# A two-layer encoder in split fp32 on one core: half of the first feed-forward group made by seven products instead of whole blocks, the forms of h made beside four blocks, and the last norm's weights scaled later

## The chip, the core and the metric

The kernel runs on one core of a Trainium2 chip. The metric is the device time of one execution in microseconds, as the median over runs; lower is better. Engines are named as the profile names them: PE (matmuls; PEld loads its stationary operand), DVE (elementwise), ACT (activations and copies), POOL (GpSimd, which here raises powers and issues the DMAs that add to what lies in memory) and SP (which issues most of the loads).

## The reference

There are two layers on x of 512 tokens by 1024 features, float32:

```python
h = rmsnorm(x, attn_norm[l]); proj = h @ w_in[l]          # 1024 -> 3072
... stick-breaking heads and differential heads ...        # mixed: 512 x 1024
x = x + mixed @ w_o[l]
h = rmsnorm(x, mlp_norm[l])
u = square(relu(h @ w_ff1[l]))                             # 1024 -> 4096
x = x + u @ w_ff2[l]                                       # 4096 -> 1024
```

After both layers comes one more `rmsnorm(x, final_norm)`. The change touches the feed-forward part (the last three lines) and the final norm.

## The kernel before

**Precision.** Every operand of a large product is split into two float32r parts, hi and lo: `hi = ACT copy(src)`, then `lo = DVE src - hi`. One product is three matmuls (`three`, L296 to L299): hi·hi, lo·hi and hi·lo. So each 512 KB tile of weights costs one ACT instruction (`whi`, L115) and one DVE instruction (`wlo`, L131) before PE can finish with it. All weight units stand in one list in the order of use (`_UNITS`); `W.next` hands out the next one and has later ones split ahead of their use.

**The feed-forward part** goes over four groups (`GROUPS`) of eight blocks of 128 hidden features in each layer. A group has two steps.

*First product, h·w_ff1.* In groups 1 to 3 it goes by seven products instead of eight: `quad_group(g, j)` runs once for each half j of the group. It takes quarters of h (256 tokens by 512 features) and quarters of the weights, or sums of these, in the order `FORMS = ("11", "x3", "x2", "21", "x1", "x4", "22")`, and each form is 24 matmuls of 128x256 into banks called X, V and Y. In group 0 of each layer the first product is made whole, by eight blocks `f0` to `f7` of 24 matmuls of 128x512 each. The reason in the code is that the forms of h (`hx`, sums and differences of quarters of h: x3, x2, 22, and x1 written over a quarter of h itself) are made only there: `h_form(k)` is called after block k, for k from 1 to 7, and `evict_whole` takes each block through relu and square and makes the seven forms of u for the second product.

*Second product, u·w_ff2.* It goes by seven products in all groups, with 128x512 matmuls into X, V, Y and W.

**Loads for the first product by seven.** `bring(n, role)` loads the quarters of half-group n. Role "a" is quarter 11, "b" is 12, "c" is 22, "d" is 21; role "e" is 12 with 22 added by a second DMA, which POOL issues with accumulation when the first has landed:

```python
quads = {"a": ("11",), "b": ("12",), "c": ("22",), "d": ("21",), "e": ("12", "22")}[role]
for q in quads:
    at = w1[_FIRST.index((l, g, j, q))]
    if q == quads[0]:
        nc.sync.dma_start(spots[role], at)
    else:
        nc.gpsimd.dma_start(spots[role], at, accum_op=ALU.add)
```

Tile `norms` holds role "e"; it also holds the sum of squares of x from which the norm before the feed-forward part is taken (`rms_square`: four transposes on PE, `rs_m`, three matmuls into the second block). Tile `waves` holds role "d". When form x3 has been split, DVE adds a to b and e to a (`add`, 128x1024 each), which gives the weights of x1 and x2.

**Order.** A scheduler that works with its own estimate of times puts the instructions of each engine in order when the program is built; each engine then runs its queue strictly in that order and waits where a semaphore asks for it. PE's queue may so hold matmuls of a later bank between those of an earlier one.

**In the last layer** `forth` transposes x back (four transposes and an ACT copy for each of eight pieces) beside the blocks of group 0, and the weights of the final norm are loaded into `gf` (two tiles of x) during form x3 of the last group's second product. `gf` is scaled by ACT (L1247, L1248, L1249) when the code has come to form x2 of that product; where these stand in ACT's queue is the scheduler's choice.

Of the kernel before, what the change touches and what calls it, by code (L numbers as in the profile page):

```python
# [12 lines left out]
AF = mybir.ActivationFunctionType  # L13
ALU = mybir.AluOpType
# [5 lines left out]
D = 1024  # L20
L = 2
# [3 lines left out]
GROUPS = 4  # L25
# [25 lines left out]
def _unit_list():  # L51
    units = []
    def qk(l, cq, ck, b):
        units.append(("p", l, cq + b * P))
        units.append(("p", l, ck + b * P))

    for l in range(L):
        for item in ORDER:
            b = int(item[1])
            if item[0] == "d":  # L60
                units.append(("x", l, b, 0))
                units.append(("x", l, b, 1))
            elif item[0] == "s":
                qk(l, SBQ, SBK, b)
            else:
                for half in range(2):
                    units.append(("v", l, (SBV if item[0] == "u" else DFV) + b * P, half))
        for half in (1, 0):
            for j in range(4):
                units.append(("o", l, half, j))  # L70
        for g in range(GROUPS):
            if g == 0:
                units.extend(("1", l, f) for f in range(2 * GP))
            else:
                units.extend(("s", l, g, j, form) for j in range(2) for form in FORMS)
            for form in FORMS2:
                for c in range(GP // 2):
                    units.append(("f", l, g, form, c))
    return units
# [9 lines left out]
_FIRST = [(l, g, j, q) for l in range(L) for g in range(1, GROUPS) for j in range(2) for q in QUADS]  # L89


class _Weights:
# [71 lines left out]
def trunk(ctx, tc, opened, xT, w, w2, w1, gfin, lamv, cos, sin, out):  # L164
# [168 lines left out]
    for l in range(L):  # L333
# [502 lines left out]
        with ExitStack() as fctx:  # L836
# [35 lines left out]
            groups = [(g, j) for g in range(1, GROUPS) for j in range(2)]  # L872
            spots = {"d": kept[(2, 1)], "e": norms.rearrange("p a t -> p (a t)")}
            serves = {"a": ("11", "x2"), "b": ("x1",), "c": ("22",), "d": ("21", "x4"), "e": ("x3",)}

# [48 lines left out]
            for g in range(GROUPS):  # L924
                for c in range(GP // 2):
# [20 lines left out]

            def evict_whole(pt, k):
                pair, which = k // 2, k % 2
                F = spots["de"[pair % 2]].rearrange("p (a t) -> p a t", a=4)
# [12 lines left out]
                split(hi[:, 3:5, :], lo[:, 3:5, :], F[:, 0:2, :])  # L962
                split_less(hi[:, 5, :], lo[:, 5, :], F[:, 2, :])
                split(hi[:, 6, :], lo[:, 6, :], F[:, 3, :])
# [11 lines left out]
                        op0=ALU.mult, op1=op)  # L976

            def h_form(k):
                if k == 1:
                    for c in range(4):  # L980
                        nc.scalar.activation(ta[:, c, :], x[:, c, early], AF.Copy, scale=gcol("mlp", l, c))
                    scaled(tb_, 0, late_, ta, ALU.subtract)
                elif k == 2:
                    scaled(tc_, 4, early, ta, ALU.subtract)
                    split(*h_forms["x3"], tb_)
                elif k == 3:
                    scaled(ta, 0, late_, tc_, ALU.add)
                elif k == 4:
                    scaled(tb_, 4, late_, ta, ALU.subtract)
                    split_less(*h_forms["x2"], ta)  # L990
                elif k == 5:
                    split_less(*h_forms["22"], tb_)
                elif k == 6:
                    for c in range(GP // 2):
                        fetch(0, "x3", c)
                elif k == 7:
                    split(*h_forms["x1"], tc_)
                    for c in range(GP // 2):
                        fetch(0, "21", c)

            def temp(k, name):
                if k == 3:
# [8 lines left out]
            def quad_group(g, j, banks_):  # L1011
# [8 lines left out]
                for form in FORMS:  # L1020
# [36 lines left out]
                    if j and form in ("11", "x3", "x2"):  # L1057
# [110 lines left out]
            for g in range(GROUPS):  # L1168
# [5 lines left out]
                    quad_group(g, 1, (s_, r_, q_))  # L1174
                    rest_of_forms(1, "21")
                else:
                    for k in range(2 * GP):
                        for n, pt in enumerate(block(f"f{l}_{g}_{k}", "any")):
                            if (k, n) == (1, 0):
                                rms_square(ssq, f"m{l}")  # L1180
                        evict_whole(pt, k)
                        h_form(k)
                        if last and k > 3:
                            for tb in (2 * (k % 2), 2 * (k % 2) + 1):
                                forth(tb, 1 - k // 6)
                    p_, q_, r_, s_ = ring[0] % 3, 3, (ring[0] + 1) % 3, (ring[0] + 2) % 3
                    held_on = {"Y": [bank("t", f"Y{l}{r}") for r in range(2)], "V": [bank("mm", f"V{l}{r}") for r in range(2)]}
                chains = {"X": [temp(k, f"X{l}{g}{k}") for k in (p_, q_)], **held_on}
                for form in FORMS2:
# [48 lines left out]
                    if g and form in ("11", "x3"):  # L1238
                        rest_of_forms(1, "x2" if form == "11" else "22")
                    if end and not last and form in ("21", "x2"):  # L1240
                        for c in range(4 * (form == "x2"), 4 * (form == "x2") + 4):
# [2 lines left out]
                        for c in range(2):  # L1244
                            nc.sync.dma_start(gf[c], gfin[512 * c : 512 * c + 512].partition_broadcast(P))
                    if end and last and form == "x2":
                        nc.scalar.activation(gf[0], gf[0], AF.Copy, scale=math.sqrt(D))  # L1247
                        nc.scalar.activation(gf[1], gf[1], AF.Copy, scale=-math.sqrt(D))  # L1248
# [101 lines left out]
```

## Time and profile before

| | |
|---|---|
| runs | 1136.55, 1139.55, 1139.09 us; median 1139.09 |
| the profiled execution, own time | 1138.57 us |
| its span | 1136.5 us, so 2.1 us lie around it |
| mean granted PE clock | 0.996 |
| busy: PE, DVE, ACT, POOL | 99%, 81%, 60%, 12% |
| group 0 of layer 0, first product | from 241.3 to 285.3 us of the span |
| group 0 of layer 1, first product | from 799.2 us; eight blocks with 32 transposes between them |

The timeline's rows are: start in us from the span's start, duration in us, engine, line, operation, what it writes and reads, shapes, how many were merged (x1), and in brackets the idle time before it with what ended that. The rows of a window are: the stretch, its length, each engine's busy time with the number of instructions, the granted PE clock, the share of the DMA engines' time and GB/s. The page's rows of DMA issues give the size of one and the median time from issue to landing.

### The profile page before, as it was taken

What the parts mean: (1) busy time and instruction counts of PE and PEld (TensorE: products, weight loads), DVE (VectorE), ACT (ScalarE), POOL (GpSimd) and SP (SyncE); (2) the same over time, 40 slices, a digit from 0 to 9 for tenths busy, and PEclk for the clock granted to TensorE, in tenths of its full rate; (3) what the DMA queues carried; (4) which work ended last, traced back from release to release, by engine and by line L of the source; (5) the groups of instructions that cost most, each with busy time, mean ns of one, the idle gap of its engine ahead of it and who ended that gap; (6) DMA issues with size and microseconds to landing.
All of it is one profiled execution on the core that took longest, in us unless ns stands there. A gap on an engine that the chain in (4) does not pass through costs nothing.

```text
span 1136.5 us, 17656 instructions
## 1 busy us (share of the span) xinstructions
PE 1122.4 (99%) x6613; PEld 992.6 (87%) x6613; DVE 914.9 (81%) x1329; ACT 687.0 (60%) x1115; POOL 137.5 (12%) x221
## 2 busy tenths in 40 slices
PE   9999999999999999999999999999999999999996
PEld 7899889888899899898888998988888998988975
DVE  7898788788669879779788877887877797797886
ACT  6456666567558457476345565675774574764763
POOL 1001343101001001001000014330010010010000
PEclk9999999999999999999999999999999999999998
DMA  7665353266877657738227544512487577567261
GB/s 250 149 187 147 93 168 112 74 207 161 234 195 165 173 163 168 204 110 224 75 78 206 162 131 130 159 65 75 167 198 199 159 167 204 149 154 216 78 128 75
DMA packets 59317, 174.99 MB, mean 154 GB/s; under 512 B 7264, under 2 KB 8544, under 8 KB 59232
## 3 DMA queue, kind: packets, MB, share of 16 engines
q1 hardware_dynamic: 50160, 141.84, 39.9%
q0 software_dynamic: 8640, 31.46, 15.8%
q8 instruction: 52, 0.85, 0.3%
q10 hardware_dynamic: 432, 0.56, 0.1%
q14 instruction: 33, 0.27, 0.1%
HBM read 144.47 MB, written 4.19 MB: 131 GB/s over the span
## 4 chain that ended last, share of the span: by engine, by line
PE 88%; DVE 5%; DMA 2%; issue 2%; ACT 1%; SPq 1%; POOL 0%; POOLq 0%; DVEq 0%; ACTq 0%
PE X L297 8%; PE X L298 8%; PE X L299 8%; PE V L297 3%; PE V L298 3%; PE V L299 3%; PE wo L297 3%; PE wo L299 3%; PE wo L298 3%; PE f L297 3%; PE f L299 3%; PE f L298 3%; PE Y L298 2%; PE Y L297 2%; PE Y L299 2%
## 5 line engine op out<-in xcount | busy, mean ns | idle before, releaser
L115 ACT ACTIVATE whi<-q 128x1024 fp32r<-128x1024 f32 x96 | 101.3, 1058 | 105.8 <-PE X L299 36.7
L131 DVE TENSOR_TENSOR wlo<-q,whi 128x1024 fp32r<-128x1024 f32 x96 | 116.9, 1221 | 42.2 <-ACT whi L115 39.1
L115 ACT ACTIVATE whi<-raw 128x1024 fp32r<-128x1024 f32 (+1 forms) x82 | 80.7, 992 | 49.6 <-issue 20.3
L131 DVE TENSOR_TENSOR wlo<-raw,whi 128x1024 fp32r<-128x1024 f32 (+1 forms) x82 | 95.2, 1168 | 10.9 <-ACT whi L115 10.5
L297 PE MATMUL X<-whi,Ah 128*128 128x512 f32 x248 | 98.2, 396 | 0.0
L298 PE MATMUL X<-wlo,Ah 128*128 128x512 f32 x248 | 97.1, 392 | 0.0
L299 PE MATMUL X<-whi,Al 128*128 128x512 f32 x248 | 96.9, 391 | 0.0
L131 DVE TENSOR_TENSOR wlo<-waves,whi 128x1024 fp32r<-128x1024 f32 x40 | 48.9, 1222 | 17.0 <-ACT whi L115 16.8
L115 ACT ACTIVATE whi<-waves 128x1024 fp32r<-128x1024 f32 x40 | 42.2, 1055 | 29.9 <-PE X L299 14.8
L297 PEld LDWEIGHTS X<-whi,Ah 128*128 128x128 f32 x248 | 46.9, 189 | 12.1 <-DVE y L1084 1.9
L299 PEld LDWEIGHTS X<-whi,Al 128*128 128x128 f32 x248 | 46.9, 189 | 10.0
L297 PE MATMUL X<-hxh,whi 128*128 128x256 f32 x192 | 54.9, 286 | 0.4 <-DVE x L1041 0.2
L298 PEld LDWEIGHTS X<-wlo,Ah 128*128 128x128 f32 x248 | 46.9, 189 | 9.0
L299 PE MATMUL X<-h_hi,wlo 128*128 128x256 f32 x192 | 54.4, 283 | 0.0
L298 PE MATMUL X<-h_lo,whi 128*128 128x256 f32 x192 | 54.4, 283 | 0.0
L298 PE MATMUL X<-hxl,whi 128*128 128x256 f32 x192 | 54.3, 283 | 0.0
L299 PE MATMUL X<-hxh,wlo 128*128 128x256 f32 x192 | 54.3, 283 | 0.0
L297 PE MATMUL X<-h_hi,whi 128*128 128x256 f32 x192 | 54.3, 283 | 0.0
L297 PE MATMUL f<-h_hi,whi 128*128 128x512 f32 x128 | 50.3, 393 | 0.0
L863 POOL DMA_DIRECT2D q<-in_w x32 | 28.7, 898 | 177.9 <-DVE wlo L131 177.9
L299 PE MATMUL f<-h_hi,wlo 128*128 128x512 f32 x128 | 49.9, 390 | 0.0
L298 PE MATMUL f<-h_lo,whi 128*128 128x512 f32 x128 | 49.8, 389 | 0.0
(740 smaller groups left out, 3819.1 us busy)
## 6 DMA issues: line engine op xcount, KB each, us to landing
raw<-in_w SPq DMA_DIRECT2D x78, 512.0 KB, 3.8
q<-in_w SPq DMA_DIRECT2D x48, 512.0 KB, 4.7
q<-in_w POOLq DMA_DIRECT2D x48, 512.0 KB, 7.5
waves<-in_w SPq DMA_DIRECT2D x28, 512.0 KB, 4.7
first_a<-in_w SPq DMA_DIRECT2D x12, 512.0 KB, 4.9
first_b<-in_w SPq DMA_DIRECT2D x12, 512.0 KB, 5.1
first_c<-in_w SPq DMA_DIRECT2D x12, 512.0 KB, 3.7
norms<-in_w SPq DMA_DIRECT2D x12, 512.0 KB, 3.6
```

Of the source, the lines that this page charges most:

```text
L115: return self.nc.scalar.activation(o, src, AF.Copy)
L131: self.last = h, nc.vector.tensor_tensor(out=lo[:, a:b], in0=raw[:, a:b], in1=hi[:, a:b].bitcast(F32), op=ALU.subtract)
L297: nc.tensor.matmul(pt, ah, bh, start=first, stop=False, skip_group_check=goes_on)
L298: nc.tensor.matmul(pt, ah, bl, start=False, stop=False, skip_group_check=goes_on)
L299: nc.tensor.matmul(pt, al, bh, start=False, stop=last, skip_group_check=goes_on)
L863: nc.gpsimd.dma_start(t, quad(g, q, c), accum_op=ALU.add)
```

## The change

Group 0 keeps four whole blocks (half 0 of the group), and its half 1 is made by `quad_group(0, 1)` as in the other groups. So the loads of its quarters move ahead of group 0, `h_form` is packed into four calls instead of seven, and `rest_of_forms` also runs for group 0. The x3 weights of that half go into `norms` right after `rms_square` has read it (`bring(0, "e")`). The first loads of w_ff2 move into `quad_group`. Lastly the three scalings of `gf` are tied behind the split that is latest at that point of the code (`in_order(W.last[0], ...)`).

```diff
         for g in range(GROUPS):
             if g == 0:
-                units.extend(("1", l, f) for f in range(2 * GP))
-            else:
-                units.extend(("s", l, g, j, form) for j in range(2) for form in FORMS)
+                units.extend(("1", l, f) for f in range(GP))
+            units.extend(("s", l, g, j, form) for j in range(g == 0, 2) for form in FORMS)
...
-            for k in (1, 2):
+            bring(0, "d")
+            for k, role in ((1, "a"), (2, "b"), (3, "c")):
                 then(("1", l, k), skip)
-            for k, role in ((5, "a"), (6, "b"), (7, "c")):
                 then(("1", l, k), bring, 0, role)
-            then(("f", l, 0, "x2", 1), bring, 0, "e")
...
-            for c in range(GP // 2):
-                fetch(0, "11", c)
...
             def h_form(k):
-                if k == 1:
+                if k == 0:
                     for c in range(4):
                         nc.scalar.activation(ta[:, c, :], x[:, c, early], AF.Copy, scale=gcol("mlp", l, c))
                     scaled(tb_, 0, late_, ta, ALU.subtract)
+                    scaled(tc_, 4, early, ta, ALU.subtract)
+                elif k == 1:
+                    split(*h_forms["x3"], tb_)
+                    scaled(ta, 0, late_, tc_, ALU.add)
                 elif k == 2:
-                    scaled(tc_, 4, early, ta, ALU.subtract)
-                    split(*h_forms["x3"], tb_)
-                elif k == 3:
-                    scaled(ta, 0, late_, tc_, ALU.add)
-                elif k == 4:
                     scaled(tb_, 4, late_, ta, ALU.subtract)
                     split_less(*h_forms["x2"], ta)
-                elif k == 5:
+                else:
                     split_less(*h_forms["22"], tb_)
...
                     split(*h_forms["x1"], tc_)
...
+                    if (g, j) == (0, 1):
+                        n = FORMS.index(form)
+                        if n < 2 and last:
+                            for tb in (2 * n, 2 * n + 1):
+                                forth(tb, 1)
+                        if n == 1:
+                            for f_, c in (("11", 0), ("11", 1), ("x3", 0), ("x3", 1), ("21", 0)):
+                                fetch(0, f_, c)
+                    elif j and form in ("11", "x3", "x2"):
...
-                    for k in range(2 * GP):
+                    for k in range(GP):
                         for n, pt in enumerate(block(f"f{l}_{g}_{k}", "any")):
                             if (k, n) == (1, 0):
                                 rms_square(ssq, f"m{l}")
+                                bring(0, "e")
                         evict_whole(pt, k)
                         h_form(k)
...
+                    quad_group(0, 1, (s_, r_, q_))
+                    rest_of_forms(1, "21")
...
                     if end and last and form == "x2":
-                        nc.scalar.activation(gf[0], gf[0], AF.Copy, scale=math.sqrt(D))
-                        nc.scalar.activation(gf[1], gf[1], AF.Copy, scale=-math.sqrt(D))
-                        nc.scalar.activation(x[:, 0, 0:256], gf[1][:, 256:512], AF.Copy, scale=r2[:, 3:4])
+                        in_order(
+                            W.last[0], nc.scalar.activation(gf[0], gf[0], AF.Copy, scale=math.sqrt(D)),
+                            nc.scalar.activation(gf[1], gf[1], AF.Copy, scale=-math.sqrt(D)),
+                            nc.scalar.activation(x[:, 0, 0:256], gf[1][:, 256:512], AF.Copy, scale=r2[:, 3:4]))
```

More of the change, by code (lines that the diff above doesn't have):

```diff
@@ L88 @@
 _QUAD = [(l, g, q, c) for l in range(L) for g in range(GROUPS) for c in range(GP // 2) for q in QUADS]
-_FIRST = [(l, g, j, q) for l in range(L) for g in range(1, GROUPS) for j in range(2) for q in QUADS]
+_FIRST = [(l, g, j, q) for l in range(L) for g in range(GROUPS) for j in range(g == 0, 2) for q in QUADS]
 class _Weights:
@@ L870, in then @@
                 W.then.setdefault(_INDEX[unit], []).append(lambda: fn(*args))
-            groups = [(g, j) for g in range(1, GROUPS) for j in range(2)]
+            groups = [(g, j) for g in range(GROUPS) for j in range(g == 0, 2)]
             spots = {"d": kept[(2, 1)], "e": norms.rearrange("p a t -> p (a t)")}
@@ L948, in evict_whole @@
                 pair, which = k // 2, k % 2
-                F = spots["de"[pair % 2]].rearrange("p (a t) -> p a t", a=4)
+                F = kept[(0, pair)].rearrange("p (a t) -> p a t", a=4)
                 hi, lo = (e[:, :, pair % 2, :] for e in sides[pair // 2])
@@ L982, in h_form @@
                     scaled(tb_, 0, late_, ta, ALU.subtract)
+                    scaled(tc_, 4, early, ta, ALU.subtract)
+                elif k == 1:
+                    split(*h_forms["x3"], tb_)
+                    scaled(ta, 0, late_, tc_, ALU.add)
                 elif k == 2:
-                    scaled(tc_, 4, early, ta, ALU.subtract)
-                    split(*h_forms["x3"], tb_)
-                elif k == 3:
-                    scaled(ta, 0, late_, tc_, ALU.add)
-                elif k == 4:
                     scaled(tb_, 4, late_, ta, ALU.subtract)
                     split_less(*h_forms["x2"], ta)
-                elif k == 5:
+                else:
                     split_less(*h_forms["22"], tb_)
[L993 to L996, printed above, removed]
                     split(*h_forms["x1"], tc_)
-                    for c in range(GP // 2):
-                        fetch(0, "21", c)
             def temp(k, name):
@@ L1056, in quad_group @@
                         nc.scalar.activation(F[3], F[3], AF.Square)
-                    if j and form in ("11", "x3", "x2"):
+                    if (g, j) == (0, 1):
[7 more added lines that the diff above has]
+                    elif j and form in ("11", "x3", "x2"):
                         rest_of_forms(0, {"11": "21", "x3": "x2", "x2": "22"}[form])
@@ L1180, in trunk @@
                                 rms_square(ssq, f"m{l}")
+                                bring(0, "e")
                         evict_whole(pt, k)
                         h_form(k)
[L1183 to L1186, printed above, removed]
+                        if last and k > 1:
+                            for tb in (2 * k - 4, 2 * k - 3):
+                                forth(tb, 0)
+                    p_, q_, r_, s_ = (ring[0] + 2) % 3, (ring[0] + 1) % 3, 3, ring[0] % 3
+                    quad_group(0, 1, (s_, r_, q_))
+                    rest_of_forms(1, "21")
                     held_on = {"Y": [bank("t", f"Y{l}{r}") for r in range(2)], "V": [bank("mm", f"V{l}{r}") for r in range(2)]}
@@ L1237, in trunk @@
                         came = gather(total, to)
-                    if g and form in ("11", "x3"):
+                    if form in ("11", "x3"):
                         rest_of_forms(1, "x2" if form == "11" else "22")
```

## The prediction

> **What bounds the kernel now.** The page comes first: busy times, the granted clock, and the chain that ended last by engine.
>
> ```profile
> span 1136.5 us, 17656 instructions
> ...
> PE 1122.4 (99%) x6613; PEld 992.6 (87%) x6613; DVE 914.9 (81%) x1329; ACT 687.0 (60%) x1115; POOL 137.5 (12%) x221
> ...
> PE 88%; DVE 5%; DMA 2%; issue 2%; ACT 1%; SPq 1%; POOL 0%; POOLq 0%; DVEq 0%; ACTq 0%
> ```
>
> PE bounds it almost everywhere, so matmul time removed is worth its full length, if the others keep PE fed. Next come the stage that is changed (layer 0's eight whole blocks, as a window) and PE's rows there: the transposes of the norm, the first matmul of block 2 and of block 3, and, from a later half-group, the first matmul of one form and of the next.
>
> ```profile
> 241.00:285.20 44.20, 44.20 (x198) 36.58 (x198) 39.64 (x68) 32.70 (x52) 4.63 (x5) 1.00 0.65 189
> ```
>
> ```profile
> 247.40 0.60 PE L283 MATMUL rs_m<-edge,norms 128*128 128x128 f32 x4
> 252.65 0.39 PE L297 MATMUL f<-h_hi,whi 128*128 128x512 f32 x1
> 258.09 0.39 PE L297 MATMUL f<-h_hi,whi 128*128 128x512 f32 x1
> 346.58 0.28 PE L297 MATMUL V<-hxh,whi 128*128 128x256 f32 x1
> 349.46 0.28 PE L297 MATMUL X<-hxh,whi 128*128 128x256 f32 x1
> ```
>
> In the window PE is busy all the time, but DVE, the third busy time, is so for 39.64 of 44.20 us: 4.6 us are free, and the change makes DVE's share denser. A block of 24 matmuls takes 258.09 - 252.65 = 5.44 us (0.227 each), a form of 24 takes 2.88 us (0.120 each).
>
> **PE's work.** Per layer four blocks go (4 x 5.44 = 21.8 us) and seven forms come (7 x 2.88 = 20.2 us): a gain of 1.6 us, 3.2 us for both layers. That is small, because twice as many matmuls of half the width save only an eighth and pay 0.120 instead of 0.113 each.
>
> **The scaling of gf.** The last group's rows, ACT first, then DVE, then PE and the window after PE's stall:
>
> ```profile
> 1081.96 1.04 ACT L1045 ACTIVATE x<-x 128x1024 f32<-128x1024 f32 x1
> 1085.81 0.63 ACT L1248 ACTIVATE x<-x 128x512 f32<-128x512 f32 x1 [2.81 <-DMA x<-in_gfin]
> 1086.35 1.04 ACT L1046 ACTIVATE x<-x 128x1024 f32<-128x1024 f32 x1
> 1087.42 1.42 DVE L945 TENSOR_TENSOR x<-x 128x512 f32<-128x512 f32 x2 [4.11 <-ACT x L1046]
> 1106.66 2.36 DVE L131 TENSOR_TENSOR wlo<-q,whi 128x1024 fp32r<-128x1024 f32 x2
> ```
>
> ```profile
> 1091.98 0.39 PE L297 MATMUL V<-whi,Ah 128*128 128x512 f32 x1
> 1093.10 0.50 PE L298 MATMUL V<-wlo,Ah 128*128 128x512 f32 x1 [0.73 <-DVE wlo L131]
> 1106.61 0.61 PE L297 MATMUL V<-whi,Ah 128*128 128x512 f32 x2
> 1109.08 0.53 PE L298 MATMUL V<-wlo,Ah 128*128 128x512 f32 x1 [1.85 <-DVE wlo L131]
> 1113.06 0.39 PE L297 MATMUL X<-whi,Ah 128*128 128x512 f32 x1
> ```
>
> ```profile
> 1093.10:1096.00 2.90, 2.90 (x13) 2.40 (x14) 2.90 (x4) 2.19 (x3) 0.86 (x1) 1.00 0.39 34
> 1109.05:1112.90 3.85, 3.82 (x10) 3.01 (x11) 3.63 (x5) 0.00 (x0) 0.00 (x0) 0.56 0.02 4
> ```
>
> ACT stands 2.81 us on the load of gf; the square behind it (L1046) starts 3.35 us after L1045 ended, and DVE, which waits for that square, has work without a break from 1087.42 until PE waits for its wlo at 1106.84. So PE waits twice, 1.12 - 0.23 = 0.9 us and then 12 matmuls in 6.45 us instead of 2.72, 3.7 us more. Of this 1.7 us is the clock (third number from the end of a window's row): 0.56 over 3.85 us. In the changed queue the scaling stands behind the splits, and the square follows at once: DVE is 3.35 us earlier, more than the two idle times together (2.6). Gain 4.6 us; bounds 0 (another wait takes over) and 4.6, taken at the upper end since the row names the releaser. Behind the later scaling wait DVE's multiplications by gf, and behind these one wlo; by then the load has landed long ago.
>
> **The new half-group in layer 0: first stall.** In the built program's order, PE's queue holds after two matmuls of block 3 the first two of X (form 11) and of V (form x3), and only then the other 22 of block 3. V's need whi of `norms`, and the third matmul of block 3 needs wlo of its own weights. `norms` is loaded only after the transposes have read it, first by SP, then by POOL adding to it. Rows of the same pair later, and the page's medians to landing:
>
> ```profile
> 296.79 0.33 SPq L886 DMA_DIRECT2D norms<-in_w x1
> 300.87 0.86 POOL L888 DMA_DIRECT2D norms<-in_w  x1 [10.21 <-DVE q L867]
> ...
> norms<-in_w SPq DMA_DIRECT2D x12, 512.0 KB, 3.6
> norms<-in_w POOLq DMA_DIRECT2D x12, 512.0 KB, 5.9
> DMA to landing us min/median/max: 3.3/4.9/8.1
> ```
>
> The transposes end at 248.0; SP issues at 248.1, 4.1 us later POOL, 5.9 us later it has landed: 258.1, say 258.3, since another load (role "b") runs beside. Bounds: 3.3 twice gives 255.3, 8.1 for the second 260.4. Queued behind SP's wait are role "b" and the first load of w_ff2, neither urgent; in POOL's queue only later additions.
>
> What hangs on that landing is more than V. In ACT's queue the copy to whi from `norms` stands ahead of two splits of u from block 1, which need nothing of it; in DVE's queue the lo parts of these stand ahead of the wlo of block 3. Prices, as starts that follow each other on each engine:
>
> ```profile
> 257.02 1.06 ACT L115 ACTIVATE whi<-raw 128x1024 fp32r<-128x1024 f32 x1 [1.67 <-DMA raw<-in_w]
> 257.98 0.40 ACT L242 ACTIVATE Ah<-waves 128x256 fp32r<-128x256 f32 x1
> ```
>
> ```profile
> 246.96 1.23 DVE L131 TENSOR_TENSOR wlo<-raw,whi 128x1024 fp32r<-128x1024 f32 x1 [1.18 <-ACT whi L115]
> ...
> 248.50 0.68 DVE L284 TENSOR_REDUCE mean<-rs_m 128x4 f32<-128x512 f32 x1
> ...
> 251.20 2.35 DVE L131 TENSOR_TENSOR wlo<-raw,whi 128x1024 fp32r<-128x1024 f32 x2
> 253.47 0.87 DVE L974 SCALAR_TENSOR_TENSOR q<-x,begin,q 128x256 f32<-128x256 f32 x2
> 254.26 0.42 DVE L945 TENSOR_TENSOR waves<-waves 128x256 f32<-128x256 f32 x1
> 255.00 1.29 DVE L238 TENSOR_TENSOR Al<-waves,Ah 128x512 fp32r<-128x512 f32 x2
> 256.20 0.42 DVE L945 TENSOR_TENSOR waves<-waves 128x256 f32<-128x256 f32 x1
> 256.54 0.48 DVE L974 SCALAR_TENSOR_TENSOR q<-x,begin,q 128x256 f32<-128x256 f32 x1
> ```
>
> DVE: 1.14 for 1024 elements, 0.60 for 512, 0.40 for a scaling by h's gain, 0.34 for other 256; ACT 0.96 for a whi. From the landing: whi 0.96 until the next starts, the split 0.41, then DVE 0.34 + 0.40 + 0.34 and the wlo 1.22, with handovers 3.8 us. So the wlo is there at 262.1. PE asks at 258.09 + 2 x 0.227 + 4 x 0.120 = 259.0: **stall 3.1 us**. Without the landing DVE's own queue from 246.96 (3 x 1.14, 2 x 0.60, 12 x 0.40, 7 x 0.34, about 0.9 for the reduction and small ones of the norm) gives 259.7: the stall is 0.7 at least.
>
> **Second stall.** X takes form x2 next; its wlo stands behind 8 x 1.14 + 2 x 0.60 + 4 x 0.40 + 7 x 0.34 = 14.3 us of DVE work after block 3's wlo (two wlo, three lo parts of h, two additions of quarters, the forms of u of blocks 2 and 3). PE has 22 x 0.227 + 48 x 0.120 = 10.8 us in that time: **stall 3.5 us**, with DVE not idle once. It is the solid part, since it is there wherever the load lands. Layer 0: 6.6 us, at the least 4.2.
>
> **Layer 1.** The same queues, but with the transposes of x between:
>
> ```profile
> 826.60 1.03 PE L1093 MATMUL xT<-edge,x 128*128 128x128 f32 x8
> ...
> 830.00 0.58 ACT L1094 ACTIVATE y<-xT 128x512 f32<-128x512 f32 x1
> ```
>
> Eight transposes take about 0.9 us. They stand in after as before (no price of their own), but give DVE time: eight before block 3 (and no X and V in it) make the first stall 2.7; three more lots make PE's stretch to the x2 weights 14.0 us, while ACT's queue gets eight copies of about 0.6 more and makes these weights 1.5 us later than DVE alone, 15.8: stall 1.8. Layer 1: 4.5 us; at the least 2.1 with the landing early, 0.6 if ACT's copies cost nothing besides.
>
> **The clock.** The stall of 1.85 us idle cost 1.7 us of clock as shown; that of 0.73 cost none (1.00). Three of the four new stalls are over 2.6 us: 3 x 1.7 = 5.1 us; the fourth, at 1.8, is left at none (up to 1.7).
> The Trainium skill (TensorE: Matmul & The Clock Gate, Part 1: The HAM clock gate) has PE fall to half rate after at least one idle window of about 3.4 us; the row shows it after 1.85 us, so the measurement decides.
>
> **Sum** against the profiled execution's 1138.57 us (span 1136.5 and 2.1 around it; the median of the runs is 0.5 higher): - 3.2 - 4.6 + 6.6 + 4.5 + 5.1 = + 8.4, **1147.0 us**.
>
> **Rivals.**
> *The clock stays up.* If gaps below about 3.4 us only halve the clock when they fall badly, as one window of fixed phase would have it, the 5.1 go: 1141.9. For it: the 0.73 row at 1.00; against it: the 1.85 row. By the Trainium skill's rule on the idle window it would go this way. Chance 0.15.
> *Not slower: the landing is no wait.* With both DMAs at the fastest row (3.3) `norms` is there at 255.3, before ACT asks (255.4 by its queue). Then 4.2 + 2.1 us of stalls remain, and with the clock up (gaps under 3.6) the sum is - 7.8 + 6.3 = - 1.5: 1137.1, same or a little faster. It decides at a landing before 255.9; against it the medians, two loads at once. Chance 0.13; a third of it beyond 0.3%, if DVE is also quicker.
> *The tail's gain fails.* ACT's copy of whi for x4 now stands behind a square that waits for DVE's gathering of Y, or the multiplication by gf holds up the wlo behind it: the 4.6 turn into a wait of the same size, 1151.6. Against it: DVE would still be 3.35 us earlier. Chance 0.10.
> That the change is not in the program is excluded: PE has 144 more matmuls in the built one (2 x (168 - 96)).
>
> **How the numbers follow.** Forecast 0.62, clock 0.15, not slower 0.13, tail 0.10. A measurement tells about 0.3%, 3.4 us, from no change, so 1135.7 to 1142.5 is "same". Faster: 0.05 of the second rival and 0.03 for what I don't see, 0.08. Same: 0.08 of the second, half of the first, 0.16. Slower: 0.76. The range reaches down to the second rival's side, 1138.0, and up to the late landing (260.4, 2 x 2.1 us) with the fourth clock drop (1.7): 1147.0 + 5.9, 1153.0.
>
> **What would show it.** In the changed profile: idle PE before a matmul of block 3 (f) released by DVE wlo in both layers, and before one of X from the x2 weights, with granted clock under 1.00 behind; ACT's whi from `norms` released by a DMA at about 258.3; DVE without idle from there on; no idle of ACT for gf, no V stall near the end. I am wrong if block 3 runs through, if `norms` lands before 256, or if the clock stays at 1.00 in both groups.

## The result and the profile after

| | before | changed |
|---|---|---|
| median of the runs, us | 1138.67 | 1151.31 |
| lowest to highest, us | 1136.55 to 1139.55 | 1150.6 to 1153.56 |
| profiled execution: own time, span, us | 1138.57, 1136.5 | 1153.56, 1151.7 |
| mean granted clock of the profiled execution | 0.996 | 0.993 |

The ratio is 1.0116, with a 95% interval of [1.0099, 1.0134]: slower by about 13 us. Forecast was 1147.0, which is 8.4 us more than the profiled execution before. The changed kernel's profiled execution is the longest of its four runs, so what follows explains 15.2 us of span, not 12.6 of medians. The page of the changed kernel, span, busy times and the chain by engine:

```profile
span 1151.7 us, 17960 instructions
...
PE 1121.4 (97%) x6757; PEld 999.0 (87%) x6757; DVE 928.8 (81%) x1329; ACT 694.3 (60%) x1115; POOL 139.3 (12%) x223
...
PE 80%; DVE 10%; DMA 5%; issue 2%; ACT 2%; POOL 0%; DVEq 0%; POOLq 0%; ACTq 0%
```

PE is busy for 1.0 us less, in a span that is 15.2 longer; in the chain, DVE and DMA have twice the share they had. The starts of PE's matmuls in the two traces say where: from block 0's first matmul to the first of half-group (1,0) layer 0 takes 10.3 us more and layer 1 10.5 more, what lies ahead, between and behind up to the last group's first products changes by less than 1 us each, and from there to PE's end it is 4.7 less.

PE's rows in the changed stage that have idle time in front of them, layer 0, then layer 1 (start, length, what, and in brackets the idle time and who ended it):

```profile
258.34 0.39 PE L296 MATMUL V<-hxh,whi 128*128 128x256 f32 x1 [0.32 <-ACT whi L114]
260.97 0.50 PE L298 MATMUL f<-h_hi,wlo 128*128 128x512 f32 x1 [2.13 <-DVE wlo L130]
...
271.88 0.39 PE L296 MATMUL X<-hxh,whi 128*128 128x256 f32 x1 [0.34 <-ACT Y L1020]
275.41 0.38 PE L298 MATMUL X<-hxh,wlo 128*128 128x256 f32 x1 [2.79 <-DVE wlo L130]
...
291.68 0.35 PE L296 MATMUL X<-hxh,whi 128*128 128x256 f32 x1 [3.50 <-DVE x L1030]
...
829.57 0.50 PE L298 MATMUL f<-h_hi,wlo 128*128 128x512 f32 x1 [2.09 <-DVE wlo L130]
...
862.38 0.55 PE L296 MATMUL X<-hxh,whi 128*128 128x256 f32 x1 [7.29 <-DVE x L1030]
```

The first two stalls are those of the prediction. The third, 3.50 and 7.29 us before form 22's first matmul into X, is in neither its sum nor its rivals. That matmul may write X once DVE has evicted x1's result from it (L1030). DVE's rows around that, in both layers:

```profile
289.10 1.23 DVE L892 TENSOR_TENSOR first_b<-first_b,first_a 128x1024 f32<-128x1024 f32 x1 [4.24 <-DMA first_a<-in_w]
290.25 0.68 DVE L237 TENSOR_TENSOR Al<-x,Ah 128x512 fp32r<-128x512 f32 x1
290.85 0.68 DVE L1030 SCALAR_TENSOR_TENSOR x<-X,x 128x512 f32<-128x512 f32 x1
...
859.80 1.23 DVE L892 TENSOR_TENSOR first_b<-first_b,first_a 128x1024 f32<-128x1024 f32 x1 [8.00 <-DMA first_a<-in_w]
860.95 0.68 DVE L237 TENSOR_TENSOR Al<-x,Ah 128x512 fp32r<-128x512 f32 x1
861.55 0.68 DVE L1030 SCALAR_TENSOR_TENSOR x<-X,x 128x512 f32<-128x512 f32 x1
```

DVE stands idle for 4.24 and 8.00 us on an addition of weights for half-group (1,0), some 40 us ahead of their use. Its operand is still being loaded, and all that DVE does for the half-group in hand is queued behind it. The loads take 8.6 to 10.2 us while many go at once (over the whole span the page has 5.5 and 5.6 for `first_b` and `first_a`); layer 0's issues between 276 and 292 us (median time to landing last):

```profile
first_b<-in_w SPq DMA_DIRECT2D x1, 512.0 KB, 9.2
first_a<-in_w SPq DMA_DIRECT2D x1, 512.0 KB, 10.2
waves<-in_w SPq DMA_DIRECT2D x1, 512.0 KB, 8.6
```

The same stretch in windows of 10 us, layer 0 and then layer 1 (busy time of PE, its loads, DVE, ACT, POOL; then the granted clock, the DMA engines' share and GB/s):

```profile
260.00:270.00 10.00, 9.03 (x55) 8.13 (x56) 10.00 (x15) 7.85 (x12) 0.88 (x1) 1.00 0.54 161
270.00:280.00 10.00, 6.87 (x43) 6.47 (x43) 8.63 (x11) 3.17 (x7) 1.73 (x2) 0.83 0.85 260
280.00:290.00 10.00, 8.18 (x69) 7.98 (x67) 4.40 (x4) 7.21 (x9) 0.87 (x1) 1.00 1.04 301
...
850.00:860.00 10.00, 5.09 (x43) 4.88 (x41) 2.00 (x3) 4.17 (x6) 0.86 (x1) 1.00 1.05 304
860.00:870.00 10.00, 7.62 (x36) 7.19 (x37) 7.82 (x10) 4.64 (x7) 1.74 (x2) 0.66 0.58 118
```

DVE's busy time falls to 4.40 and to 2.00 us of 10 in just those windows in which the DMA engines are taken all the time (share 1.04 and 1.05). In these stages the clock is reduced twice, after the second stall of layer 0 (from 276.31, for 3.41 us) and after the third of layer 1 (from 859.99, for 6.83 us).

The tail came out as forecast: in the last group ACT's square follows the Relu at once, DVE waits 0.81 us for it (4.11 before), and the scaling of gf comes 20 us later, when nothing waits for it:

```profile
1102.27 1.04 ACT L1034 ACTIVATE x<-x 128x1024 f32<-128x1024 f32 x1
1103.35 1.06 ACT L1035 ACTIVATE x<-x 128x1024 f32<-128x1024 f32 x1
...
1124.79 0.61 ACT L1248 ACTIVATE x<-x 128x512 f32<-128x512 f32 x1
```

```profile
1104.44 1.42 DVE L941 TENSOR_TENSOR x<-x 128x512 f32<-128x512 f32 x2 [0.81 <-ACT x L1035]
```

### The profile page after: what moved, and what is told of

It is laid out like the page before. It is cut to its first block, busy times and chain, and to the rows that moved or that the text cites. A ratio compares the mean times of both kernels' runs of the same rounds, so it can differ in the third digit from the quotient of the medians.

```text
span 1151.7 us, 17960 instructions
## 1 busy us (share of the span) xinstructions
PE 1121.4 (97%) x6757; PEld 999.0 (87%) x6757; DVE 928.8 (81%) x1329; ACT 694.3 (60%) x1115; POOL 139.3 (12%) x223
## 4 chain that ended last, share of the span: by engine, by line
PE 80%; DVE 10%; DMA 5%; issue 2%; ACT 2%; POOL 0%; DVEq 0%; POOLq 0%; ACTq 0%
PE X L296 8%; PE X L297 8%; PE X L298 8%; DVE wlo L130 3%; PE V L296 3%; PE V L297 3%; PE V L298 3%; DMA first_a<-in_w 2%; PE Y L296 2%; PE Y L297 2%; PE Y L298 2%; PE wo L296 2%; PE wo L297 2%; DMA first_b<-in_w 2%; PE wo L298 2%
## 5 line engine op out<-in xcount | busy, mean ns | idle before, releaser
L130 DVE TENSOR_TENSOR wlo<-raw,whi 128x1024 fp32r<-128x1024 f32 (+1 forms) x74 | 85.8, 1163 | 11.0 <-ACT whi L114 10.5
L296 PE MATMUL X<-hxh,whi 128*128 128x256 f32 x224 | 65.7, 293 | 12.5 <-DVE x L1030 12.1
L298 PE MATMUL X<-hxh,wlo 128*128 128x256 f32 x224 | 65.1, 291 | 2.9 <-DVE wlo L130 2.8
L297 PE MATMUL X<-hxl,whi 128*128 128x256 f32 x224 | 64.9, 290 | 0.0
L114 ACT ACTIVATE whi<-waves 128x1024 fp32r<-128x1024 f32 x44 | 46.4, 1055 | 29.7 <-PE X L298 13.2
L296 PE MATMUL X<-h_hi,whi 128*128 128x256 f32 x224 | 63.4, 283 | 0.0
L297 PE MATMUL X<-h_lo,whi 128*128 128x256 f32 x224 | 63.4, 283 | 0.0
L237 DVE TENSOR_TENSOR Al<-x,Ah 128x512 fp32r<-128x512 f32 (+1 forms) x70 | 54.2, 791 | 3.0 <-ACT Ah L236 2.7
L296 PEld LDWEIGHTS X<-hxh,whi 128*128 128x128 f32 x224 | 44.5, 199 | 13.6 <-issue 11.1
L298 PEld LDWEIGHTS X<-whi,Al 128*128 128x128 f32 x248 | 46.5, 188 | 9.9
L236 ACT ACTIVATE Ah<-x 128x512 fp32r<-128x512 f32 (+1 forms) x70 | 49.4, 708 | 4.7 <-DVE x L941 4.2
L114 ACT ACTIVATE whi<-first_a 128x1024 fp32r<-128x1024 f32 x28 | 29.7, 1059 | 36.0 <-PE V L297 10.9
```

The source lines that it names most:

```text
L114: return self.nc.scalar.activation(o, src, AF.Copy)
L130: self.last = h, nc.vector.tensor_tensor(out=lo[:, a:b], in0=raw[:, a:b], in1=hi[:, a:b].bitcast(F32), op=ALU.subtract)
L236: a = nc.scalar.activation(hi, src, AF.Copy)
L237: nc.vector.tensor_tensor(out=lo, in0=src, in1=hi.bitcast(F32), op=ALU.subtract)
L296: nc.tensor.matmul(pt, ah, bh, start=first, stop=False, skip_group_check=goes_on)
L297: nc.tensor.matmul(pt, ah, bl, start=False, stop=False, skip_group_check=goes_on)
```

## The experiments

Times are medians; the ratio is to runs of the kernel before on the same chip, with its 95% interval in brackets. The kernel before took 1137.0 to 1137.5 us beside these runs and 1138.67 beside the changed kernel, so a difference to 1151.31 is good to a us or two. Line numbers shift by a few from kernel to kernel.

**1. The tail alone.** The kernel before with this edit:

```diff
-    nc.scalar.activation(gf[0], ...); nc.scalar.activation(gf[1], ...); nc.scalar.activation(x[:, 0, 0:256], ...)
+    in_order(W.last[0], nc.scalar.activation(gf[0], ...), nc.scalar.activation(gf[1], ...), ...)
```

> The kernel before with only the later scaling of the last norm's weights. Theory (the two parts of the change add up; the trace of after shows the tail 4.7 us shorter and the two group-0 stages 20.9 us longer): no stall of V near the end and no half clock there, 1138.6 - 4.7 = 1134 us (1132.5 to 1135.5). Rival (the tail came out shorter only because the new group 0 shifted the weights' arrival): 1138 to 1139 us, with the stall of 3.7 us still there.

Measured: 1133.56 us, ratio 0.9969 [0.9957, 0.998]; the span is 4.6 us shorter, without a stall of V near the end and with no half clock ahead of PE's last microseconds. So the gain does not need the new group 0.

**2. The new group 0 alone.** The changed kernel with that edit undone.

> The changed kernel with the old scaling of the last norm's weights. Theory: 1151.3 + 4.7 = 1156 us, with the stalls of V at the end back. Rival (the tail was not what gave the 4.7 us): 1151 to 1152 us.

Measured: 1156.45 us, ratio 1.0171 [1.0156, 1.0186]. V's stalls are back (0.32 and 1.81 us idle). The tail is worth 1156.45 - 1151.31 = 5.1 here and 3.6 in the first run. The two parts add up to within 3 us: + 19.3 and - 3.6, each against the kernel before in its own set, give + 15.7, and the whole change measured + 12.6.

**3. The addition later in DVE's queue.**

```diff
     def add(to, by, n=0):
         step = nc.vector.tensor_tensor(out=spots[to], in0=spots[to], in1=spots[by], op=ALU.add)
+        if n == 1:
+            behind(step, passed[0])
 ...
-                        tt2(F[2], F[2], F[1], ALU.add)
+                        passed.append(tt2(F[2], F[2], F[1], ALU.add))
```

> The changed kernel, the addition first_b += first_a of half-group (1,0) put in DVE's queue behind the last eviction step of form x4 of half-group (0,1) instead of ahead of the eviction of x1. Theory (the third stall of each layer is DVE's queue standing behind the loads of the next half-group): the stalls of 3.65 and 7.45 us go to under 1 us each, and the half clock of layer 1 (1.9 us) with them: 1151.3 - 13.0 = 1138.3, at most 1141 with what is late next. The first stalls (2.29, 2.26 us) and layer 0's second (2.94 us) stay as they are. Rival (the many loads under way at that time are late themselves, and others of them hold up PE instead): stalls of the same size under another name, 1147 to 1151 us.

Measured: 1141.99 us, ratio 1.0037 [1.0024, 1.005]; 9.3 us less than the changed kernel. The third stalls are gone in both layers; nothing takes their place. DVE's rows in layer 0:

```profile
284.80 0.68 DVE L1034 SCALAR_TENSOR_TENSOR x<-X,x 128x512 f32<-128x512 f32 x1
...
296.72 1.22 DVE L894 TENSOR_TENSOR first_b<-first_b,first_a 128x1024 f32<-128x1024 f32 x1
```

The eviction no longer stands behind the addition, and the addition, 12 us after it, waits for nothing. So the order in the queue was the cause. The profiled execution took 1139.32 us, within the theory's range; the median is above it, and nine runs spread from 1138.88 to 1145.45 us, the longer ones mostly at the lower granted clock (0.997 down to 0.990). More on that below: the stalls of 2.1 to 2.8 us that remain reduce the clock in one execution and not in the next.

**4. x3's weights earlier, into another tile.** Besides the edit of run 3:

```diff
+            spare = y[(1, 1)].rearrange("p a t -> p (a t)")
+                if role == "e":
+                    spots["e"] = norms.rearrange("p a t -> p (a t)") if n else spare
 ...
+                if k == 1:
+                    then(("1", l, k), bring, 0, "e")
```

> As the run before, and the two loads of form x3's weights of half-group (0,1) go into y's tile of row block (1,1), free until then, some 3 us earlier, instead of into norms after the norm's sums have been read; the same loads for (1,0) stand behind first_c. Theory (block 3's third matmul waits on that landing): the first stalls fall from 2.8 and 2.3 us to under 0.7 each, and DVE, which starts its queue 3 us earlier, is less late for x2 (layer 0: 3.45 to about 1 us), so that layer 0's half clock goes too: 1138.3 - 4 - 2.5 - 1.5 = 1130 us (1129 to 1134). Rival (DVE's own queue is the bound, the landing hides behind it): the first stall keeps at least half, the second all: 1136 to 1139 us.

Measured: 1143.34 us, ratio 1.006 [1.0048, 1.0072]. Neither expectation held: the second stall is whole (3.5 us), as the rival has it, but the first is longer than before, not shorter (3.65 us between PE's starts in layer 0, 2.70 in layer 1). ACT's rows:

```profile
256.20 1.06 ACT L114 ACTIVATE whi<-y 128x1024 fp32r<-128x1024 f32 x1 [3.58 <-DMA y<-in_w]
257.17 0.61 ACT L963 ACTIVATE q<-q 128x512 f32<-128x512 f32 x1
```

The second load landed only 1.0 us earlier: the first was issued 2.0 us earlier (245.11 against 247.11), not 3, and took 4.5 us instead of 3.6; and the scheduler, which counted on more, put whi's copy also ahead of the square of block 1's output (L963), so that more of DVE's work hung on the same landing.

**5. One load instead of two for x3's weights.** Run 3, with the accumulating load left out for (0,1). Form x3 of that half-group then multiplies by quarter 12 alone, so this kernel computes something else and serves only to time the landing.

```diff
-                    else:
+                    elif (n, role) != (0, "e"):
                         nc.gpsimd.dma_start(spots[role], at, accum_op=ALU.add)
```

> The run with the later addition, and of the two loads into norms for form x3 of half-group (0,1) the second, accumulating one is left out (form x3 then multiplies by half of its weights), so that norms lands some 6.5 us earlier. The built order also sets block 3's low part some places earlier in DVE's queue. Theory of the prediction (block 3's third matmul waits behind that landing, by way of ACT's and DVE's queues): the first stalls, 0.5 + 2.3 us in layer 0 and 2.4 in layer 1, go to under 0.7 and 0.3; 1142.0 - 4.3 = 1137.7, and to 1135 if DVE, started earlier, is also in time for x2. Rival (DVE's own work is the bound and the landing is hidden by it): at least 1.5 us stays in each layer, 1140 to 1142.

Measured: 1134.97 us, ratio 0.9977 [0.9968, 0.9987], 7.0 us less than run 3. The first stalls are gone in both layers; layer 0's second one is whole (3.5 us), so the landing makes no difference to it. Two things moved for the first: the landing, and, as the expectation says, block 3's low part in DVE's queue. How much is due to each comes below.

**6. Block 3's parts later.** Run 3, and after the Relu and square of block 3 the rest of its eviction is written behind form x3.

```diff
+                    if k == 3:
+                        return
 ...
+                        if n == 1:
+                            evict_whole(None, 3, True)
```

> The run with the later addition, and the differences and low parts of block 3's own output (some 5 us of DVE, needed only for the second product) stand in the program behind form x3 instead of ahead of the forms; loads as they are. Theory of the prediction (x2's low part stands in DVE's queue behind work that PE doesn't need yet): layer 0's second stall, 0.5 + 2.9 us, goes to under 0.7, and the half clock that follows it with it; the first stalls stay: 1142.0 - 3 - 1 = 1138 (1136.5 to 1139.5). Rival (x2 waits for the sum of its weights, so for the landing of norms, whatever DVE does besides): the second stall keeps over 2 us, 1140.5 to 1142.

Measured: 1153.17 us, ratio 1.0141 [1.0124, 1.0158], 11.2 us more than run 3. The second stall is gone, as the theory has it, but PE waits later and longer, PE's row and ACT's:

```profile
296.71 0.79 PE L296 MATMUL X<-whi,Ah 128*128 128x512 f32 x1 [7.15 <-ACT whi L114]
```

```profile
295.61 1.06 ACT L114 ACTIVATE whi<-q 128x1024 fp32r<-128x1024 f32 x1 [8.65 <-DMA q<-in_w]
```

Block 3's output lies in the tile into which the second product's weights are loaded next. The parts came later, so did the tile's release, and a load issued at 282.4 landed at 295.6, 13.2 us later, while the other loads of that time took 7 to 14 us. The edit moved the price instead of removing it.

**7. Both, and x3's loads still earlier.** Run 6 with run 4's tile, its load ahead of the last three stores of x and of first_a in SP's queue.

```diff
+                    if c > 4:
+                        behind(parked, begun[0, "e"])
 ...
+                        if (n, role) == (0, "a"):
+                            behind(begun[n, role], begun[0, "e"])
```

> Later addition, block 3's parts later, and form x3's weights loaded into y's tile ahead of the last three stores of x to DRAM and ahead of first_a in SP's queue (the run with x3 early had it behind first_a, and there the second load landed only 1.0 us earlier than in the changed kernel, 256.18 against 257.20, with the first stall as long as before). Theory: if the second load lands by 253 the first stalls go to under 0.7 us, the second too, and the gain of PE's work (3.2) and of the tail (4.7) is left: 1137.2 - 3.2 - 4.7 + 1.5 = 1131 (1129.5 to 1134), below the run with the tail alone (1133.56). Rival (the tile's memory comes free too late, so that the load can't start before 244 and only delays first_a and the stores behind it): 1137 to 1142.

Measured: 1145.67 us, ratio 1.0077 [1.0054, 1.0099]: the rival, and worse. SP's rows:

```profile
244.96 0.33 SPq L891 DMA_DIRECT2D y<-in_w  x1
245.34 1.43 SPq L953 DMA_DIRECT2D park<-x  x3
246.82 0.63 SPq L891 DMA_DIRECT2D first_a<-in_w  x1
```

Though first in its queue, the load starts at 244.96, 0.15 us earlier than in run 4; now three stores and first_a go at the same time, and PE waits 4.8 us for a low part that form 11 needs (`X<-h_hi,wlo`).

**8. x3's weights into waves.** Run 3, with two tiles exchanged for (0,1): form x3's weights ("e", two loads) into waves, form 21's ("d", one load) into norms. The loads into norms for (1,0) are called for after form x4 instead of x3.

```diff
-            bring(0, "d")
+            bring(0, "e")
 ...
-                                bring(0, "e")
+                                bring(0, "d")
```

> The run with the later addition, and two tiles of half-group (0,1) change places: form x3's weights, which need two loads one after the other, go into waves, free since the attention's start, and form 21's, which need one, into norms after the sums have been read. Nothing is left out. Theory (the first stalls are the landing in norms, as the run with one load showed at 1134.97): the first stalls go in both layers, the second of layer 0 stays at 3 to 3.5 us, 1135 (1133.5 to 1136.5). Rival (in the run with one load it was the missing traffic that helped, not the early landing): 1138 to 1142.

Measured: 1143.51 us, ratio 1.0058 [1.0041, 1.0074]. Both first stalls are gone with no traffic left out, and the second is 3.5 us: the stages up to the second product take 48.8 us in layer 0 and 46.5 in layer 1, to 0.1 as long as in run 5. So it was not the missing traffic. But 8.5 us are lost elsewhere: 1.4 at 89 us, where PE waits for DMA, and 5.3 in layer 1's second product, which takes 43.7 us by PE's starts instead of 38.4; the rest lies in small waits between. ACT's rows in that product:

```profile
866.84 1.06 ACT L114 ACTIVATE whi<-q 128x1024 fp32r<-128x1024 f32 x1 [6.08 <-DMA q<-in_w]
870.17 1.07 ACT L114 ACTIVATE whi<-q 128x1024 fp32r<-128x1024 f32 x1 [2.27 <-DMA q<-in_w]
```

There the load into norms for (1,0) now stands in GpSimd's queue ahead of three that the second product needs.

**9. Sums on GpSimd.** Run 8, and the two sums of (0,1) with `nc.gpsimd` instead of `nc.vector`.

> The run with x3's weights in waves, and the two sums of weights of half-group (0,1) (first_b += first_a, first_a += waves; 2 x 1.14 us of DVE's queue ahead of x2's low part) made by GpSimd, which is idle then. Theory (the second stall is DVE's amount of work, DVE being busy without a gap from 250 to 270 us): layer 0's second stall goes from 3.5 to 1 to 1.5 us, mostly without a half clock behind it: 1132.5 (1131 to 1134). Rival (GpSimd's sum of 128x1024 is so slow, or holds DVE up so much, that x2's weights are later than before): the stall stays at 3 us or grows, 1135 to 1140.

Measured: 1147.80 us, ratio 1.0088 [1.0071, 1.0104], 4.3 us more than run 8: the rival's mechanism. PE waits again before block 3 (1.94 us in layer 0, 1.05 in layer 1), 2.89 and 1.92 us around form x2 in layer 0, and 4.18 us in layer 1. GpSimd's rows:

```profile
254.48 3.11 POOL L898 TENSOR_TENSOR first_b<-first_b,first_a 128x1024 f32<-128x1024 f32 x1 [41.28 <-DMA first_b<-in_w]
267.50 4.99 POOL L898 TENSOR_TENSOR first_a<-first_a,waves 128x1024 f32<-128x1024 f32 x1 [9.90 <-DVE wlo L130]
```

3.11 and 4.99 us stand against 1.14 on DVE. And DVE is slower beside it; three scalings by h's gain, in this run and in run 8:

```profile
255.34 3.33 DVE L978 SCALAR_TENSOR_TENSOR q<-x,begin,q 128x256 f32<-128x256 f32 x3
```

```profile
254.79 1.25 DVE L977 SCALAR_TENSOR_TENSOR q<-x,begin,q 128x256 f32<-128x256 f32 x3
```

2.1 us more in the time of one sum, about what the move was to save in all. The Trainium skill (SBUF — State Buffer, SBUF: two separate sides) says that a DVE instruction with two SBUF inputs and a GpSimd instruction that reads SBUF share a port pair, which the first to start holds to its end. The trace agrees: the first of the three scalings, started at 255.34, ends at 257.88, just behind GpSimd's sum (254.48 + 3.11 = 257.59), and the other two take 0.4 each. Beside the second sum it is the other way round: DVE's three instructions from 268.33 to 270.22 keep their usual 0.4 and 1.2 us, and the sum takes 4.99.

**10. Run 8 without its side costs.**

```diff
+    behind(added, W.weighing)        # (0, "e"): behind the attention's last multiplication on GpSimd
 ...
+    behind(added, queued["POOL"])    # (1, "e"): behind the second product's accumulating loads
 ...
+    behind(begun, queued["SP"])      # (1, "e"): the same in SP's queue
```

> The run with x3's weights in waves, with its two side costs taken out: the accumulating load into waves stands in GpSimd's queue behind the attention's last multiplication (there it came early and the queue waited for the first load: PE lost 1.4 us at 89 us), and the loads of half-group (1,0) into norms stand behind those of the second product's weights (there the second product of layer 1 lost 5.2 us to late weights). Theory: the first stalls stay away, the second of layer 0 stays at 3.5 us, and 1143.5 - 1.4 - 1.0 - 5.2 = 1136 (1134 to 1138). Rival (the time goes wherever the next load is late, the DMA queues being full from 270 to 300 us): 1140 to 1144.

Measured: 1134.03 us, ratio 0.9967 [0.9955, 0.998], 9.5 us less than run 8 by the places of these three loads alone. One stall of some size is left:

```profile
272.50 0.58 PE L298 MATMUL X<-hxh,wlo 128*128 128x256 f32 x1 [3.38 <-DVE wlo L130]
```

What gave back the time at 89 us, the place in GpSimd's queue or the traffic that moved with it, these runs do not separate.

**11. And block 3's parts later in layer 0, from a tile that nobody waits for.**

```diff
+                if pair and not last:
+                    F = y[(1, 1)].rearrange("p a t -> p (a t)").rearrange("p (a t) -> p a t", a=4)
 ...
+                    if k == 3 and not last:
+                        return
```

> The run above, and in layer 0 alone blocks 2 and 3 put their output into y's tile of (1,1), and block 3's differences and low parts stand behind form x3 (the run that did this in both layers, with the output in the second product's own tile, lost 7.3 us to the weights that had to wait for that tile). Theory (the second stall is DVE's work ahead of x2's low part): layer 0's second stall goes and the half clock with it, 1136 - 3.5 - 1.5 = 1131 (1129.5 to 1133.5), below the run with the tail alone (1133.56). Rival (what is moved comes back as a stall of the second product): 1135 to 1139.

Measured: 1130.75 us (1129.33 to 1132.94), ratio 0.9942 [0.9929, 0.9955]: the fastest version, 6.7 us below the kernel before and 2.8 below the tail alone (which ran on another chip; by the two ratios it is 3.1). The window rows of layer 0 and PE's only stall there:

```profile
270.00:280.00 10.00, 9.56 (x78) 9.16 (x77) 10.00 (x14) 6.65 (x12) 0.87 (x1) 1.00 0.93 252
280.00:290.00 10.00, 10.00 (x66) 9.12 (x65) 8.85 (x13) 8.24 (x11) 2.59 (x3) 1.00 1.05 299
```

```profile
270.71 0.39 PE L298 MATMUL Y<-h_hi,wlo 128*128 128x256 f32 x1 [0.44 <-DVE wlo L130]
```

DVE and the DMA queues are as full as in the changed kernel (10.00 of 10 us, share 1.05), PE runs through, and the clock stays at 1.00.

## Why the prediction was right, and where it was wrong

The direction was right and so were most of its mechanisms; the size was short by 4.3 us, because one large term was missing and others were too large.

- **PE's work, -3.2.** It fits: with the stalls all but out, run 11 gains 2.8 us on the tail alone (3.1 by the ratios).
- **The scaling of gf, -4.6.** Right in mechanism: run 1 gains 3.6 by medians and 4.6 by spans. The rival that the gain fails is out, though its time, 1151.6, is nearly the one measured (1151.31): by the number alone the wrong cause would have been picked.
- **First stall, 3.1 and 2.7.** Right in mechanism: ACT's copy of `norms`, released by the DMA, starts at 257.23, with 258.3 forecast for a stage that now begins 0.9 earlier. Sizes 0.32 + 2.13 and 2.09 us idle. ACT's idle time before that copy puts the rival "the landing is no wait" out:

```profile
257.23 1.06 ACT L114 ACTIVATE whi<-norms 128x1024 fp32r<-128x1024 f32 x1 [2.83 <-DMA norms<-in_w]
```

  In runs 5, 8 and 10 the landing is early and the stall is gone. That does not refute the bound of 0.7 by DVE's own queue, since their built order is another one: three short instructions of DVE (3 x 0.34 = 1.0 us) that stood ahead of block 3's wlo stand behind it, and so do PE's four matmuls of X and V (0.5 us). Run 5's rows show how close it is even so:

```profile
256.71 1.22 DVE L130 TENSOR_TENSOR wlo<-raw,whi 128x1024 fp32r<-128x1024 f32 x1
257.98 0.50 PE L298 MATMUL f<-h_hi,wlo 128*128 128x512 f32 x1
```

  The wlo ends at 257.93 and PE takes it at 257.98. With the old order about 0.5 us of stall would be left, by an estimate from these numbers (1.0 - 0.5); some 2 us of it were the landing.

- **Second stall, 3.5 and 1.8.** Layer 0's is right (0.34 + 2.79) and independent of the landing, as "the solid part" said; run 11 removed it by DVE's order. Layer 1's was under 0.4 us: DVE took 14.2 us there from the end of block 3's wlo to the end of x2's, as in layer 0 (14.4), where 15.8 was forecast. The eight copies of ACT's queue, priced at 1.5 us more, cost nothing on the path.
- **The clock, three drops of 1.7.** The size of one is about right, the number is not. Of the three only the drop after layer 0's second stall came; the first stalls, at 2.1 us, lowered nothing in this execution (in run 2's, layer 0's first one did). The other drop followed the third stall. PE's matmuls of 128x256 start 0.20 to 0.21 us apart in the two reduced stretches instead of 0.12, which costs 1.5 and 2.0 us. The rival "the clock stays up" did not come, but the fixed phase that it speaks of is what the traces show (last section).
- **The missing term.** The step that failed is the end of the queue reading: DVE's instructions were counted up to x2's wlo and "DVE without idle from there on" was put down as a sign. Seven instructions further in the same queue stood the next half-group's addition, with its wait for a load. Its price, 3.50 + 7.29 us idle and a drop of the clock, is what the sum lacked (run 3: 9.3 by medians). In the kernel before, DVE waits at such additions too, and PE has work meanwhile:

```profile
334.52 1.23 DVE L893 TENSOR_TENSOR first_b<-first_b,first_a 128x1024 f32<-128x1024 f32 x1 [2.77 <-DMA first_b<-in_w]
```

  The one for (1,0) waited for nothing there (274.43). That a wait is harmless before a change says nothing of it after a move.

That the forecast lay no further off is luck. In the profiled executions, by PE's starts, the third stalls cost 3.7 + 7.5 us and 2.0 of clock, about 13 us for which the sum had nothing. Against that stood three terms that were too large: the first stalls by 0.9, layer 1's second stall by 1.5 and the clock at the places forecast by 3.6 (5.1 against 1.5), about 6 us together.

## To carry to other kernels

When a change makes a stage denser, read each in-order queue to the end of the stage and not to the first wait that counts: an instruction for later work that waits for a load blocks all that the present work has queued behind it. Find for each added transfer the tile's release, the queue and the other transfers of that moment; here the places of three loads were worth 9.5 us, and a tile that others were waiting for cost a stall of 7. A stall once located is removed by order or place, and what is then late next is read from the new trace before the next edit.

## What the runs showed of the hardware

The clock's fall goes by a fixed grid. In each execution the starts of reduced clock lie whole multiples of 3413.3 ns apart: 171.00 in the changed kernel (276.31 and 859.99 us), 5.00 and 175.00 in run 2. Every trace has at least one such start (after PE's last matmul at the latest), which fixes the grid for it. Laid over PE's idle times it gives:

| window of 3.41 us from | PE idle in it, us | clock in the next |
|---|---|---|
| changed, 272.90 (second stall) | 2.51 | 0.5 |
| changed, 259.25 (first stall) | 1.72 | 1.0 |
| changed, 286.55 and 289.97 (third stall, cut by the grid) | 1.78 and 1.71 | 1.0 |
| changed, 825.86 (first stall, layer 1) | 1.79 | 1.0 |
| run 3, 823.77 (first stall, layer 1) | 1.80 | 1.0 |
| run 3, 270.81 and 274.22 (second stall, cut by the grid) | 1.52 and 1.60 | 1.0 |
| before, 1106.00 (V near the end) | 1.85 | 0.5 |
| run 2, 1125.70 (the same) | 1.81 | 0.5 |

In all traces together, between PE's first 10 us and its end and outside the reduced stretches themselves, 20 windows had 1.81 us or more of idle PE, and half clock followed all of them; of those below, it followed one (1.57, in run 7). The profile models the ends of matmuls, so the border between 1.80 and 1.81 is not that sharp. So it takes a window that is idle for about half or more, and a stall of 2 to 3.6 us falls into one or is cut in two, as the grid's phase in that execution has it. Run 3's second stall and the changed kernel's are the same 2.8 us; one lost its clock and one did not. It fits that run 3, with such stalls, spreads over 6.6 us and run 11, without, over 3.6; the grid of the executions without a trace is not known. The Trainium skill (TensorE: Matmul & The Clock Gate, Part 1: The HAM clock gate) describes a free-running window of 3413 ns; the traces agree to the nanosecond. That section of the Trainium skill asks for at least one idle window; the rows show half clock after 1.81 us of idle time in one, so the measurement decides.

The second unexpected thing is what a sum on GpSimd does to DVE: beside one of 3.11 us, three DVE instructions took 3.33 instead of 1.25 us, and beside the other no DVE instruction was slower, but the sum took 4.99 us (run 9).
